# A new instruction order for a 9000-instruction encoder kernel: same work, other places in the queues

## The chip, the cores and the metric

One core of a Trainium2 chip runs the whole kernel as one program. The metric is the time of one execution on the device in microseconds (us). Before the change it was 1069.17 us, the median of 3 runs (1068.3 to 1069.39). The profile shown below comes from one more execution, with its own time.

## The reference: one layer of a hybrid encoder

The input x has 512 rows (the sequence) of 1024 columns, all in float32. What must come out is

```python
h = rmsnorm(x, mix_norm)
p = h @ w_in                                   # 1024 -> 9248 columns
rx, ry, qkv, z, ba, gates = split(p)
y_rnn = rglru_branch(rx, ry, ...) @ w_rnn_proj # 12 blocks of 128 channels, conv of 4, two gates, scans both ways
y_dn  = deltanet_branch(qkv, z, ba, ...) @ w_dn_proj   # 8 heads, chunked delta rule, both ways
g_rnn, g_dn = split(sigmoid(gates))
x = x + (g_rnn * y_rnn + g_dn * y_dn) @ w_out
gt, up = split(rmsnorm(x, ffn_norm) @ w_gate_up)       # 2 x 2816 columns
x = x + (silu(gt) * up) @ w_down
return rmsnorm(x, final_norm)
```

## The kernel before

**Products.** A float32 matrix product is made of three products of a faster type, `float32r`. Each operand is split into a high part (a cast) and a low part (the operand minus its high part). For weights the tiles are called `whi` and `wlo`, for the normalised x `hh` and `hl`; the kernel adds `whi*hh`, `whi*hl` and `wlo*hh` in PSUM. ScalarE makes the casts, VectorE the subtractions, TensorE the products and the transposes. `stage` loads a raw weight tile (`wraw`, three buffers, mostly 512 KB) on SyncE's (SP's) queue, casts it and subtracts. `whi` and `wlo` have two buffers each. PSUM has three buffers `mm`, three `ax` and two `st`.

**Stages.** Two chunks of 128 rows of x are loaded, squared and summed, scaled (half of the columns on VectorE, half on ScalarE), transposed on TensorE into `ax` and evicted as `hh` (ScalarE) and `hl` (VectorE); then the other two chunks (`norm_scale`, `norm_transpose`). From then on the blocks of the recurrent branch (`rg_front`, `rg_exp`, `rg_rest`, `rg_out`: Sigmoid, Tanh and Exp, Sqrt, Gelu), the heads of the delta branch (`dn_front`, `dn_mats`, `dn_inverse`, `dn_state`: Silu, Square, Sqrt, Exp, small 32x32 and 64x64 products) and the output projections run mixed with one another until some 690 us; then the FFN, whose gate/up and down products use seven products of quarter size instead of eight, and the final norm. The first `wraw` tiles are numbers 265 (cast 266, subtraction 267) and 451 (cast 452). Number 113 loads the weights of beta and the decay gates, 32 columns of `w_in`, so its pieces in DRAM are 128 bytes long (cast 114). The first two chunks of x are numbers 8 and 9, the others 55 and 56.

**What sets the order.** The functions do not emit instructions. Every call goes through `Rec`, which notes engine, function, sources and estimated durations with `Plan.add`, and numbers the instructions from 0 to 8999. All 9000 therefore have line 704 in the profile. At the end the list `ORDER` says in which order they are emitted:

```python
with tc.manual_schedule():
    todo = plan.order()
    for i in todo:
        plan.ops[i][1]()
```

`Plan.order` only checks that the list holds each number once and no use ahead of its source. Each engine works off its own instructions in the order in which they are emitted, so `ORDER` fixes five queues: TensorE (5973 instructions), VectorE (1578), ScalarE (1064, eleven of them DMA issues), GpSimd (89, nine of them DMA issues) and SP (296, all DMA issues). Between engines, semaphores make an instruction wait for its sources; an instruction that waits holds up everything behind it on its queue. The durations in `Rec.__getattr__` and the sets in `Plan.TABLES` are not read when the kernel runs.

**ScalarE's tables.** Exp, Sigmoid, Sqrt, Ln, Silu and Gelu sit in different table sets. Where the next function on the queue is not in the loaded set, the compiler puts an `ACT_TABLE_LOAD` ahead of it. Copy, Square, Identity and Abs need none, Tanh is in several sets. How many loads there are is thus a matter of ScalarE's order alone.

Of the kernel before, what the change touches and what calls it, by code (L numbers as in the profile page):

```python
# [31 lines left out]
    8, 10, 9, 265, 111, 110, 99, 112, 100, 2, 5, 101, 0, 103, 104, 106, 102, 1, 5475, 13, 14, 15, 3, 7, 18, 17, 19,  # L32
    266, 16, 39, 11, 12, 20, 21, 22, 267, 31, 23, 24, 25, 26, 29, 27, 30, 28, 32, 33, 34, 35, 36, 37, 38, 40, 41,
    42, 43, 44, 45, 46, 47, 48, 49, 50, 51, 53, 52, 54, 55, 57, 58, 56, 62, 59, 60, 451, 452, 63, 64, 268, 269, 270,
    271, 107, 272, 273, 274, 275, 276, 277, 278, 279, 280, 281, 282, 283, 105, 284, 285, 286, 287, 288, 289, 108,
    290, 291, 454, 455, 456, 457, 458, 459, 460, 65, 67, 68, 75, 76, 69, 316, 317, 318, 319, 453, 66, 61, 70, 77,
    73, 78, 71, 81, 79, 74, 72, 109, 82, 80, 461, 462, 463, 464, 465, 466, 467, 468, 469, 470, 471, 472, 473, 474,
    475, 83, 84, 85, 86, 91, 92, 93, 94, 87, 89, 88, 95, 90, 96, 97, 98, 292, 293, 476, 477, 294, 295, 296, 297,
    298, 299, 478, 300, 301, 302, 303, 304, 305, 306, 307, 187, 583, 502, 503, 504, 188, 308, 309, 310, 311, 312,
    313, 314, 315, 479, 480, 505, 320, 481, 482, 483, 484, 190, 191, 192, 193, 485, 486, 487, 488, 489, 194, 195,  # L40
    490, 196, 197, 491, 492, 493, 198, 199, 200, 201, 494, 495, 202, 203, 204, 205, 496, 497, 498, 499, 500, 321,
    322, 323, 189, 324, 325, 239, 238, 501, 334, 206, 240, 241, 113, 114, 506, 326, 335, 338, 339, 327, 328, 207,
    340, 208, 341, 329, 209, 210, 211, 212, 213, 214, 215, 216, 217, 507, 508, 115, 509, 510, 511, 336, 337, 330,
    331, 332, 333, 218, 219, 220, 221, 222, 223, 224, 116, 117, 118, 225, 226, 227, 228, 512, 229, 119, 529, 584,
    585, 611, 610, 612, 613, 520, 230, 231, 521, 522, 523, 120, 232, 233, 234, 586, 587, 235, 236, 237, 242, 243,
    516, 121, 122, 513, 514, 123, 124, 524, 588, 125, 126, 517, 518, 519, 244, 245, 246, 525, 526, 589, 515, 395,
    394, 343, 396, 342, 247, 397, 527, 528, 127, 128, 129, 130, 131, 132, 133, 590, 591, 134, 256, 135, 136, 137,
    138, 248, 249, 250, 139, 140, 141, 142, 143, 592, 144, 145, 146, 147, 344, 251, 148, 345, 257, 252, 593, 594,
    595, 258, 259, 253, 596, 597, 598, 599, 346, 600, 601, 149, 150, 151, 152, 260, 153, 158, 556, 557, 558, 160,
    154, 155, 159, 559, 161, 530, 347, 348, 254, 261, 349, 262, 350, 263, 264, 351, 352, 602, 603, 353, 604, 605,  # L50
    354, 532, 533, 606, 607, 608, 609, 255, 531, 162, 614, 163, 165, 166, 615, 787, 788, 789, 790, 616, 617, 355,
    356, 357, 358, 359, 360, 534, 535, 536, 361, 537, 538, 539, 540, 362, 363, 364, 365, 541, 542, 366, 367, 368,
    369, 370, 371, 372, 373, 374, 375, 376, 377, 378, 379, 380, 381, 382, 383, 384, 385, 386, 171, 164, 618, 624,
    387, 388, 389, 390, 391, 392, 167, 168, 169, 170, 173, 172, 174, 393, 175, 6, 176, 177, 4, 178, 179, 619, 625,
    628, 629, 630, 1076, 1077, 398, 399, 181, 760, 841, 842, 843, 180, 626, 631, 627, 1079, 543, 544, 545, 400, 401,
    844, 402, 546, 632, 633, 634, 620, 183, 621, 622, 547, 184, 548, 623, 635, 412, 403, 413, 414, 415, 761, 762,
    416, 417, 418, 419, 636, 420, 404, 405, 549, 406, 407, 550, 551, 408, 409, 410, 411, 422, 425, 421, 1080, 1081,
    552, 763, 553, 554, 764, 765, 766, 555, 1082, 767, 768, 769, 1083, 1084, 1085, 1086, 770, 1087, 1088, 1089,
    1090, 1091, 771, 772, 430, 560, 432, 426, 561, 562, 563, 564, 565, 1078, 773, 1092, 774, 775, 776, 777, 778,
    779, 574, 780, 781, 1093, 1094, 782, 566, 575, 576, 783, 895, 896, 424, 423, 1045, 897, 429, 431, 1046, 567,  # L60
    784, 785, 786, 568, 791, 428, 427, 569, 577, 898, 1047, 792, 793, 794, 795, 796, 1095, 1096, 1097, 1048, 1049,
    1050, 1098, 1099, 1051, 1052, 1100, 1053, 1054, 1101, 1102, 1055, 1056, 1057, 1058, 1059, 1060, 578, 579, 570,
    571, 572, 1200, 637, 1103, 1104, 1105, 1106, 1201, 1202, 805, 580, 581, 582, 573, 1061, 806, 807, 1062, 1063,
    808, 433, 439, 638, 185, 1064, 1203, 809, 810, 1204, 1205, 1206, 1207, 801, 1065, 1208, 1209, 1210, 797, 1066,
    802, 1211, 1067, 1068, 1212, 1213, 1069, 1070, 1071, 434, 440, 435, 437, 639, 436, 441, 442, 445, 446, 1214,
    640, 641, 798, 799, 642, 643, 1215, 1216, 1072, 800, 1217, 644, 1218, 645, 803, 804, 646, 647, 1219, 648, 814,
# [1850 lines left out]
```

## Time and profile before

| | before |
|---|---|
| median of 3 runs | 1069.17 us |
| the profiled execution's own time | 1068.94 us |
| its span | 1067.2 us |
| TensorE busy | 1043.8 us, 98% |
| VectorE busy | 897.2 us, 84% |
| ScalarE busy | 680.5 us, 64% |
| GpSimd busy | 48.8 us, 5% |
| ScalarE table loads | 71 |

The span runs from the first to the last instruction; 1.74 us of the execution's time lie outside it. Busy time of TensorE counts bars that overlap: a matmul's bar lasts longer than the distance to the next one's start, so that a busy TensorE need not be one at its full pace. In a row, the part behind `[` is the idle time ahead of the instruction on its engine and what ended it. Names of tiles stand without buffer numbers.

### The profile page before, as it was taken

Reading aid. Unit: us, or ns where it says so; the run is one execution under the profiler, and the core shown is the slowest. Engines: PE = TensorE matmul, PEld = TensorE weight load, DVE = VectorE, ACT = ScalarE, POOL = GpSimd, SP = SyncE. Lnnn points to the kernel's source line nnn. Section 1 sums busy time; section 2 is a strip of 40 time slices with the busy share of each in tenths; the row PEclk is TensorE's granted clock in tenths of the full one; section 3 lists DMA queues with packets and bytes.
Section 4 is the critical chain, followed back from the end, with each engine's and each line's share of the span. In section 5 each row is a group of like instructions: output and inputs, shape, how many; then the busy total and the mean of one; then the engine's idle time right before and its main releaser. Section 6 shows DMA issues by size and latency. Waiting matters only on the chain.

```text
span 1067.2 us, 17684 instructions
## 1 busy us (share of the span) xinstructions
PE 1043.8 (98%) x6730; PEld 907.4 (85%) x6730; DVE 897.2 (84%) x1584; ACT 680.5 (64%) x1235; POOL 48.8 (5%) x93
## 2 busy tenths in 40 slices
PE   6999999999999999999999999999999999999997
PEld 5888887888877978898888878889999999998785
DVE  5668899779997999889949957879889998899877
ACT  6698899898447756857855453438444545355656
POOL 2000002010300100210200000000000000000000
PEclk9999999999999999999999999999999999999999
DMA  6343333236645756453221322632333433336564
GB/s 183 85 109 100 99 95 114 80 117 203 184 117 164 266 168 212 130 180 99 60 57 40 89 66 88 180 99 80 99 99 100 119 99 90 110 116 194 168 220 162
DMA packets 174053, 134.36 MB, mean 126 GB/s; under 512 B 6096, under 2 KB 152704, under 8 KB 173968
## 3 DMA queue, kind: packets, MB, share of 16 engines
q1 hardware_dynamic: 172416, 129.91, 41.2%
q10 hardware_dynamic: 1264, 3.19, 0.9%
q8 instruction: 53, 0.87, 0.4%
q0 software_dynamic: 288, 0.13, 0.2%
q14 instruction: 32, 0.26, 0.1%
HBM read 119.55 MB, written 13.66 MB: 125 GB/s over the span
## 4 chain that ended last, share of the span: by engine, by line
PE 56%; DVE 4%; ACT 2%; DMA 1%; issue 1%; DVEq 0%; ACTq 0%
PE mm L704 30%; PE ax L704 17%; PE st L704 9%; DVE t L704 2%; ACT t L704 1%; DVE wlo L704 1%; DMA wraw<-in_w_out_dram 1%; DVE na L704 1%; DMA wraw<-dsum 0%; ACT whi L704 0%; DMA wraw<-in_w_dn_proj_dram 0%; ACT L704 0%; ACT ax L704 0%; DVE hh L704 0%; DVE so L704 0%
## 5 line engine op out<-in xcount | busy, mean ns | idle before, releaser
L704 DVE TENSOR_TENSOR t<-t,t 128x512 fp32r<-128x512 f32 (+21 forms) x480 | 251.8, 536 | 33.1 <-ACT t L704 24.1
L704 PE MATMUL mm<-hh,whi 128*128 128x512 f32 (+2 forms) x704 | 241.3, 357 | 1.8 <-ACT whi L704 1.1
L704 ACT CAST whi<-wraw 128x1024 fp32r<-128x1024 f32 (+3 forms) x171 | 165.5, 970 | 120.1 <-PE mm L704 57.4
L704 PE MATMUL mm<-hl,whi 128*128 128x512 f32 (+2 forms) x704 | 241.1, 355 | 0.1
L704 DVE TENSOR_TENSOR wlo<-wraw,whi 128x1024 fp32r<-128x1024 f32 (+3 forms) x170 | 191.2, 1128 | 47.6 <-ACT whi L704 36.1
L704 PE MATMUL mm<-hh,wlo 128*128 128x512 f32 (+1 forms) x688 | 174.6, 354 | 0.0
L704 PEld LDWEIGHTS mm<-hh,whi 128*128 128x128 f32 (+1 forms) x704 | 132.6, 189 | 21.5 <-ACT whi L704 2.2
L704 PEld LDWEIGHTS mm<-hl,whi 128*128 128x128 f32 (+1 forms) x704 | 133.0, 189 | 17.6 <-DVE hl L704 0.3
L704 PEld LDWEIGHTS mm<-hh,wlo 128*128 128x128 f32 x688 | 120.9, 189 | 17.9 <-DVE wlo L704 0.3
L704 PE MATMUL ax<-t,t 32*32 32x32 f32 (+3 forms) x870 | 115.2, 263 | 2.2 <-issue 1.0
L704 ACT CAST t<-t 128x512 fp32r<-128x512 f32 (+3 forms) x117 | 74.7, 653 | 48.4 <-DVE t L704 45.1
L704 ACT ACT_TABLE_LOAD x71 | 91.1, 1283 | 9.6 <-PE mm L704 4.6
L704 PEld LDWEIGHTS ax<-t,t 128*128 128x128 f32 (+1 forms) x870 | 82.8, 153 | 11.2 <-ACT t L704 3.1
L704 PE MATMUL mm<-t,whi 128*128 128x512 f32 x320 | 90.7, 395 | 0.3 <-DVE t L704 0.3
L704 DVE SCALAR_TENSOR_TENSOR t<-mm,par,t 128x511 f32<-128x511 f32 (+1 forms) x108 | 80.2, 745 | 9.8 <-ACT t L704 8.5
L704 PE MATMUL mm<-t,t 128*128 128x256 f32 (+1 forms) x348 | 78.1, 313 | 0.1
L704 PEld LDWEIGHTS mm<-t,whi 128*128 128x128 f32 x320 | 59.3, 188 | 13.7 <-DVE t L704 0.9
L704 PEld LDWEIGHTS mm<-t,t 128*128 128x128 f32 x348 | 58.0, 191 | 4.2 <-ACT t L704 0.4
L704 ACT ACTIVATE t<-t 128x128 f32<-128x128 f32 (+4 forms) x84 | 45.6, 555 | 20.7 <-DVE t L704 20.0
L704 PE MATMUL mm<-t,wlo 128*128 128x512 f32 x160 | 48.9, 393 | 0.0
L704 PE MATMUL ax<-whi,t 128*128 128x512 f32 x137 | 48.3, 392 | 0.2 <-ACT whi L704 0.2
L704 PE MATMUL st<-hh,whi 128*128 128x512 f32 (+1 forms) x112 | 41.7, 377 | 0.0
(211 smaller groups left out, 1817.3 us busy)
## 6 DMA issues: line engine op xcount, KB each, us to landing
wraw<-in_w_in_dram SPq DMA_DIRECT2D x72, 512.0 KB, 4.0
wraw<-in_w_gate_up_dram SPq DMA_DIRECT2D x44, 512.0 KB, 3.9
t<-in_w_down_dram SPq DMA_DIRECT2D x22, 512.0 KB, 5.0
dsum<-t SPq DMA_DIRECT2D x22, 512.0 KB, 5.2
wraw<-dsum SPq DMA_DIRECT2D x20, 512.0 KB, 3.9
wraw<-in_w_down_dram SPq DMA_DIRECT2D x15, 512.0 KB, 4.0
wraw<-in_w_rnn_proj_dram SPq DMA_DIRECT2D x16, 384.0 KB, 3.6
t<-gsum SPq DMA_DIRECT2D x16, 256.0 KB, 4.5
```

The lines of the kernel that those rows point to most:

```text
L704: self.plan.add(e, lambda: real(*a, **kw), outs, ins, occ, lat, tail, table, mode)
```

## The change

Only the list `ORDER` is replaced, lines 31 to 520; every function stays as it is, and so do the 9000 instructions and their numbering. The beginning of the list:

```diff
 ORDER = [
-    8, 10, 9, 265, 111, 110, 99, 112, 100, 2, 5, 101, 0, 103, 104, 106, 102, 1, 5475, 13, 14, 15, 3, 7, 18, 17, 19,
-    266, 16, 39, 11, 12, 20, 21, 22, 267, 31, 23, 24, 25, 26, 29, 27, 30, 28, 32, 33, 34, 35, 36, 37, 38, 40, 41,
-    42, 43, 44, 45, 46, 47, 48, 49, 50, 51, 53, 52, 54, 55, 57, 58, 56, 62, 59, 60, 451, 452, 63, 64, 268, 269, 270,
...
+    9, 8, 265, 2, 99, 6, 0, 5, 111, 103, 102, 104, 100, 105, 18, 10, 1, 19, 112, 110, 4, 106, 3, 101, 20, 21, 7, 22,
+    13, 14, 15, 16, 17, 11, 12, 266, 267, 23, 24, 25, 26, 27, 28, 29, 30, 31, 32, 33, 34, 35, 37, 36, 38, 39, 40,
+    41, 42, 43, 44, 45, 46, 268, 47, 48, 49, 50, 51, 53, 52, 54, 451, 113, 452, 55, 57, 56, 583, 316, 317, 62, 63,
...
```

Read by queues, this is what the places named later come to. The lists are cut to one engine each; `+` is the new order of the same queue.

```diff
 SP, from the start
-  8 (x0), 9 (x1), 265 (wraw), 55 (x2), 56 (x3), 451 (wraw), 316, 317 (graw), 187 (wraw), 583 (wraw)
+  9 (x1), 8 (x0), 265 (wraw), 451 (wraw), 113 (wraw, 32 columns), 55 (x2), 56 (x3), 583 (wraw), 316, 317 (graw), 187 (wraw)
 ScalarE, from the start
-  10, 1, 5475, 13 (Square x0), 14 (Sqrt), 17 (scale x0), 19 (Sqrt), 266 (cast), 22 (scale x1), 29, 27, 35, 37 (hh)
+  10, 1, 19 (Sqrt), 22 (scale x1), 13 (Square x0), 14 (Sqrt), 17 (scale x0), 266 (cast), 27, 29, 35, 37 (hh)
 ScalarE, around the Sigmoid at 67.30 us of the old profile
-  398 (Identity), 843 (cast), 180 (Exp), 631, 627 (Sigmoid), 402 (cast)
+  180 (Exp), 396 (cast), 398 (Identity), 627, 631 (Sigmoid), 402 (cast)
 ScalarE, around the Silu at 183.00 us
-  1013 (cast), 1233, 1234 (Silu), 1495 (cast)
+  1329 (cast), 1495 (cast), 1599 (Identity), 1232, 1233 (Silu)
 ScalarE, around the cast at 386.44 us
-  2492 (Square), 2496 (Sqrt), 2888 (copy of na), 3368 (cast whi), 3363, 2886
+  2486, 2490 (Square), 3368 (cast whi), 2882, 2888 (copies of na)
 ScalarE, around the cast at 564.81 us
-  3960, 4941 (Sigmoid), 5028 (cast whi), 4001
+  3960, 4941 (Sigmoid), 5028 (cast whi), 4001
```

On GpSimd's queue the mask `upi`, from which VectorE makes the identity for the transposes, moves behind eight of the nine DMA issues. On SP's queue 211 of 296 entries change places, by 3.0 places on average; on TensorE's 2776 of 5972 pairs of neighbours stay neighbours, on VectorE's 298 of 1577, on ScalarE's 161 of 1063. The last 17 instructions of TensorE are the same.

970 rows, old and new, of the table ORDER are left out of this document.

## The prediction, made before the result was known

> **What bounds the kernel now.** I read the page's totals first, then busy time by stretches, TensorE's waits, the groups of instructions by form, and last the timelines around each wait.
>
> ```profile
> span 1067.2 us, 17684 instructions
> ...
> PE 1043.8 (98%) x6730; PEld 907.4 (85%) x6730; DVE 897.2 (84%) x1584; ACT 680.5 (64%) x1235; POOL 48.8 (5%) x93
> ...
> PE 56%; DVE 4%; ACT 2%; DMA 1%; issue 1%; DVEq 0%; ACTq 0%
> ```
>
> TensorE is busy 98% of the span, and in the chain that ended last VectorE has only 4% and ScalarE 2%. The change removes no matmul, so at most 1067.2 − 1043.8 = 23.4 us of its visible idle time is open to it, and a new order can only move that idle time. The stretches show where it lies (columns: stretch, length, then busy us and count of TensorE, its weight loads, VectorE, ScalarE, GpSimd, then clock, DMA share, GB/s).
>
> ```profile
> 7.50:27.00 19.50, 17.05 (x103) 15.00 (x104) 14.87 (x33) 13.11 (x29) 1.41 (x3) 1.00 0.67 177
> ...
> 100.00:200.00 100.00, 99.57 (x435) 80.93 (x434) 90.86 (x105) 90.44 (x120) 5.59 (x3) 1.00 0.34 96
> ...
> 700.00:1000.00 300.00, 300.00 (x2221) 287.17 (x2220) 265.37 (x447) 153.82 (x270) 0.00 (x0) 1.00 0.38 112
> ...
> 1059.00:1067.20 8.20, 0.30 (x2) 0.00 (x0) 3.99 (x12) 3.29 (x10) 0.00 (x0) 0.71 0.38 133
> ```
>
> Of the 23.4 us, 19.50 − 17.05 = 2.45 lie between 7.5 and 27 us and 8.20 − 0.30 = 7.9 after 1059 us, in the final norm; up to 7.5 lie ahead of 7.5 us, while x is loaded. The stretch from 700 to 1000 us, in the FFN, has none. What is left between 27 and 1059 us is a handful of waits:
>
> ```profile
> PE mm L704 <- ACT whi L704: 1.6, 3, 0.6
> PE ax L704 <- issue: 1.0, 1, 1.0
> PE ax L704 <- ACT t L704: 0.9, 1, 0.9
> PE ax L704 <- DVE t L704: 0.6, 3, 0.3
> PE mm L704 <- DVE t L704: 0.6, 2, 0.3
> ```
>
> ScalarE causes 1.6 + 0.9 = 2.5 us of these in four waits, VectorE 0.6 + 0.6 = 1.2 us in five. An idle time shown is less than what the wait costs, because a matmul's bar overlaps the next one:
>
> ```profile
> 385.86 0.39 PE L704 MATMUL mm<-hh,whi 128*128 128x512 f32 x1
> ...
> 386.54 0.39 PE L704 MATMUL mm<-hl,whi 128*128 128x512 f32 x1
> 387.54 0.50 PE L704 MATMUL mm<-hh,whi 128*128 128x512 f32 x1 [0.61 <-ACT whi L704]
> 387.87 0.39 PE L704 MATMUL mm<-hl,whi 128*128 128x512 f32 x1
> ```
>
> Three starts take 386.54 − 385.86 = 0.68 us, so the pace is 0.227 us. The wait made 1.00 us of it, 0.77 lost against 0.61 shown, and the next start took 0.33, another 0.10. I count waits by starts below.
>
> **The change part by part.** Every instruction stays, only places in the five queues move: 5507 of TensorE's 5973, 1400 of VectorE's 1578, 932 of ScalarE's 1064, by 10.6, 5.4 and 7.2 places on average.
>
> *ScalarE's table loads.* Counting along ScalarE's queue how often the function leaves the loaded set gives 70 for the old list and 60 for the new one (Exp 21 to 15, Sigmoid 17 to 14, Sqrt 14 to 13).
>
> ```profile
> L704 ACT ACT_TABLE_LOAD x71 | 91.1, 1283 | 9.6 <-PE mm L704 4.6 <-DVE so L704 2.5 <-PEq L1903 1.4
> ```
>
> The trace has 71, so the count is right to one. Ten fewer at 1283 ns are 12.8 us less ScalarE work. But ScalarE is busy 64%, so nearly all of it falls into its idle time and is worth nothing; it counts only where TensorE waits behind a load. There are three places where the new list takes away what was in front of the late ScalarE result. At 387.54 us, the weights' high half (number 3368) came late:
>
> ```profile
> 382.69 1.28 ACT L704 ACT_TABLE_LOAD   x1 [2.05 <-DVE so L704]
> ...
> 386.01 0.40 ACT L704 COPY t<-na 32x256 f32<-32x256 f32 x1 [1.72 <-DVE na L704]
> 386.44 1.04 ACT L704 CAST whi<-wraw 128x1024 fp32r<-128x1024 f32 x1
> ```
>
> It stood behind a Sqrt with its table load and behind a copy that waited 1.72 us for VectorE's `na`. In the new list cast 3368 stands directly ahead of these `na` copies and the Sqrt (2496) is no longer among the six instructions ahead of it: 0.77 us gone. At 68.04 us:
>
> ```profile
> 66.29 0.84 PE L704 MATMUL ax<-t,t 128*128 128x512 f32 x3
> 68.04 0.49 PE L704 MATMUL ax<-t,t 128*128 128x512 f32 x1 [0.91 <-ACT t L704]
> ```
>
> ```profile
> 64.36 1.28 ACT L704 ACT_TABLE_LOAD   x1
> 65.66 0.33 ACT L704 ACTIVATE ge<-ax 128x192 f32<-128x192 f32 x1
> 66.00 1.28 ACT L704 ACT_TABLE_LOAD   x1
> 67.30 1.26 ACT L704 ACTIVATE t<-ax,par 128x512 f32<-128x512 f32 x2
> ```
>
> The last of the three starts at 66.29 + 0.84 − 0.39 = 66.74, so the wait cost 68.04 − 66.74 − 0.227 = 1.07 us. The gate's Exp sits between two loads right ahead of the Sigmoid; in the new list a graw cast (396) and a conv start (398) lie between Exp (180) and Sigmoid, and the Exp comes earlier against TensorE. I take the whole 1.07. At 185.16 us:
>
> ```profile
> 184.21 0.84 PE L704 MATMUL mm<-hh,wlo 128*128 128x512 f32 x3
> 185.16 0.50 PE L704 MATMUL ax<-t,t 128*128 128x512 f32 x1
> ```
>
> The last start of the three is 184.66, so 185.16 − 184.66 − 0.227 = 0.27 us; the cast it needs (1495) stood behind a Silu load with two Silus and now stands ahead of them. Sum: 0.77 + 1.07 + 0.27 = **2.1 us**. A wait that stays is this one:
>
> ```profile
> 563.02 1.28 ACT L704 ACT_TABLE_LOAD   x1 [4.63 <-PE mm L704]
> 564.32 0.60 ACT L704 ACTIVATE t<-mm 128x512 f32<-128x512 f32 x1
> 564.81 1.04 ACT L704 CAST whi<-wraw 128x1024 fp32r<-128x1024 f32 x1
> ```
>
> Sigmoid 4941 and cast 5028 are neighbours in both lists. Bounds for the stage between 27 and 1059 us: if all nine ScalarE and VectorE waits went, 2.5 + 1.2 shown, with 0.77 − 0.61 = 0.16 hidden in each and 0.10 behind each as at 387.54, that is 3.7 + 9 × 0.26 = 6.0 us gained. The other end is a loss: one VectorE instruction (90.86 / 105 = 0.87 us) more in front of TensorE in seven places, 6.1 us. I stay at the three waits whose cause the list visibly removes.
>
> *The head.* The first weight cast went ahead of the copy that scales the second 128 rows of x:
>
> ```profile
> 10.00 1.04 ACT L704 CAST whi<-wraw 128x1024 fp32r<-128x1024 f32 x1 [1.32 <-DMA wraw<-in_w_in_dram]
> 10.95 0.72 ACT L704 ACTIVATE t<-t,rin 128x512 f32<-128x512 f32 x1
> ...
> 16.23 1.06 ACT L704 ACTIVATE t<-t 128x1024 f32<-128x1024 f32 x1
> ```
>
> ScalarE idled 1.32 us for the weights, and then the copy, the transposes and ScalarE's evictions `hh` ran late, for which VectorE waited:
>
> ```profile
> 14.23 0.88 DVE L704 SCALAR_TENSOR_TENSOR hl<-ax,gain,hh 128x256 fp32r<-128x256 f32 x2 [0.54 <-ACT hh L704]
> 15.65 0.48 DVE L704 SCALAR_TENSOR_TENSOR hl<-ax,gain,hh 128x256 fp32r<-128x256 f32 x1 [0.54 <-ACT hh L704]
> 16.38 0.87 DVE L704 SCALAR_TENSOR_TENSOR hl<-ax,gain,hh 128x256 fp32r<-128x256 f32 x2 [0.25 <-ACT hh L704]
> ```
>
> The new list has both scaled copies ahead of that cast. VectorE's weight subtraction still comes before its first `hl`, so what can go are its three waits: 0.54 + 0.54 + 0.25 = **1.3 us** earlier for the last `hl` and the matmuls that read it. The upper end is all of TensorE's idle time there, 2.45 us; the lower one is the transfers. SP's queue now issues a second 512 KB weight tile and the 128 KB beta/gate weights (number 113) ahead of rows 2 and 3 of x.
>
> ```profile
> DMA packets 1124, 0.57 MB, mean 283 GB/s; under 512 B 29, under 2 KB 1122, under 8 KB 1124
> ```
>
> That is the stretch from 12 to 14 us: the x rows come in 4 KB pieces and almost none are left, so they had landed by about 12 us. The added 0.524 MB at 283 GB/s are 1.9 us, and the 0.131 MB between 0.5 us at the same rate and 3.3 us at 40 GB/s, the slowest slices that moved much in the old list's stretch with this load (26 to 34 us, slices of 0.2 us):
>
> ```profile
> GB/s 0 0 0 0 0 0 0 0 0 0 0 13 172 338 261 164 284 158 139 184 129 40 40 27 19 0 0 0 0 0 0 0 0 0 0 0 44 113 108 95
> DMA packets 1724, 0.47 MB, mean 58 GB/s; under 512 B 1072, under 2 KB 1724, under 8 KB 1724
> ```
>
> So the rows land between 14.4 and 17.2 us. The Square of them started at 16.23 and should start at 14.9: covered at the near end, up to 2.3 us late at the far one, which would turn 1.3 us of gain into 1.0 of loss. Most slices of that stretch ran at 129 to 338 GB/s, so I take the near end. Behind x, SP's third weight buffer is now taken, so the next weight load waits until VectorE has subtracted the first tile, as SP's queue did before.
>
> The Trainium skill, "DMA: Bandwidth & Descriptors" (Specifications), wants at least 512 B a piece for full rate; the beta/gate load has 128 B pieces, and the 1072 small packets in the slow slices agree. By that rule the head loses 1.0 and the sum would be 1067.8.
>
> *GpSimd and the end.* GpSimd's mask for the identity now follows eight DMA issues; I put the identity at the same 7 to 8 us, between 0.3 late and nothing. In the last 8.2 us the 17 final TensorE instructions keep their order, two ScalarE ones swap: 0, within ±0.2.
>
> *Sum*, against the profiled execution, 1068.94 us (span 1067.2 and 1.74 around it, 0.2 under the median of 1069.17): 1068.94 − 2.1 − 1.3 = **1065.5 us**.
>
> **The rivals.** *Nothing gained* (about 1068.3): the waits only change places. For it: 5507 moved places leave few neighbours as they were, and ScalarE's 36% idle time swallows table loads. Each of the three waits is replaced by one of its like and the head alone gives half, 1068.94 − 0.6. Against: each of the three has lost its visible cause. *Late x rows*: the far end above, 1068.94 − 2.1 + 1.0 = 1067.8. *Most waits go* (about 1061.6): 1068.94 − 1.3 − 6.0 = 1061.6. For it, no wait beyond 27 us exceeds 1.0 us; against, neighbours such as 4941 and 5028 stay.
>
> *VectorE becomes the bound* (about 1071.6, slower): from 100 to 200 us VectorE is busy 90.86 us and has 9 us to spare. The new list places its work in other blocks against TensorE's. If TensorE asks for a result one VectorE instruction earlier than it is ready, that is 0.87 us; seven places cost 6.1, and 1068.94 − 3.4 + 6.1 = 1071.6. It decides from four places on (3.4 / 0.87), where the gain is used up. Against: VectorE causes only 1.2 us of TensorE's waits now, at 91% busy in this stretch.
>
> **How the numbers follow.** Forecast 0.42, its own range 1064 to 1067 (half the three waits, or the head's upper end); nothing gained 0.16; late x rows 0.10; most waits go 0.13; VectorE 0.19. A measurement here tells about 0.2%, 2.1 us, from no change: faster is under 1067.0, slower over 1071.3. Faster: 0.41 of the forecast's, 0.13 and 0.02 of the late rows', 0.56. Slower: VectorE's share and 0.01 of the second, 0.20. The same: 0.24. The range 1060.5 to 1071.5 leaves out half of VectorE's case and the end of the best, about 0.15.
>
> **What would show it.** Right: 61 table loads; no `ACT whi` wait at the group that began at 387.54, none on `ACT t` at the one at 68.04; the first `hh` before 11.2 us and the last of the eight `hl` ending near 15.9 instead of 17.25. Wrong: x's second Square waiting for a DMA past 16 us; `PE <- DVE wlo` or `DVE t` rows of several us between 100 and 500 us, or TensorE's waits in the middle summing to 4.7 us again.

## The result, and the profile after

The new list takes 1059.62 us (median of 4 executions, 1059.15 to 1060.07) against 1068.76 us (1068.3 to 1069.39) for the old one, which has one execution more here than in the table ahead: a ratio of 0.9914, 95% interval 0.9897 to 0.9931, or 9.1 us less. The forecast was 1065.5 us and its range began at 1060.5, so the sign was right and the gain was more than twice the size forecast. The profiled execution took 1060.07 us, its span is 1058.3 us, 8.9 less than before.

The page's totals after, the chain that ended last, and the group of table loads:

```profile
span 1058.3 us, 17715 instructions
...
PE 1037.6 (98%) x6730; PEld 910.3 (86%) x6730; DVE 897.5 (85%) x1584; ACT 665.9 (63%) x1225; POOL 49.1 (5%) x93
...
PE 64%; DVE 7%; issue 1%; ACT 1%; POOL 0%; DMA 0%; DVEq 0%; POOLq 0%
...
L704 ACT ACT_TABLE_LOAD x61 | 78.3, 1283 | 3.2 <-PEq L1903 1.4
```

The loads are down from 71 to 61 as counted. TensorE has the same 6730 instructions, and yet its busy time fell by 6.2 us, from 1043.8 to 1037.6. A matmul that is held up gets a longer bar, not only an idle time in front of it (0.50 us against 0.39 at 387.54 us in the prediction's rows); the waits view sees only the second.

The stretches after (columns as in the prediction), and below them one of before that it did not show:

```profile
100.00:200.00 100.00, 100.00 (x443) 82.81 (x442) 92.90 (x108) 89.24 (x119) 0.03 (x1) 1.00 0.36 98
...
300.00:400.00 100.00, 100.00 (x730) 85.36 (x729) 87.39 (x193) 65.11 (x152) 1.24 (x2) 1.00 0.58 184
...
700.00:1000.00 300.00, 299.59 (x2219) 286.65 (x2218) 269.43 (x450) 158.32 (x275) 0.00 (x0) 1.00 0.38 112
...
1050.40:1058.30 7.90, 0.18 (x1) 0.00 (x0) 4.12 (x13) 3.33 (x10) 0.00 (x0) 0.84 0.47 162
```

```profile
300.00:400.00 100.00, 98.94 (x720) 82.82 (x719) 87.97 (x183) 62.96 (x145) 4.46 (x10) 1.00 0.56 176
```

The counts of TensorE's instructions tell more than its busy time: in the same hundred microseconds it now does 8 more (100 to 200 us) and 10 more (300 to 400). As one list runs ahead of the other, the same hundred microseconds do not hold quite the same instructions; the table further down compares at equal work. The FFN and the last 7.9 us are as they were. The granted clock is 1.00 in all of these but the last.

TensorE's waits between 27 and 1050 us after (us in total, times, longest):

```profile
PE mm L704 <- DVE t L704: 1.6, 2, 1.0
PE mm L704 <- ACT hh L704: 0.5, 1, 0.5
PE mm L704 <- ACT whi L704: 0.5, 1, 0.5
PE ax L704 <- ACT whi L704: 0.4, 1, 0.4
PE ax L704 <- POOL t L704: 0.3, 1, 0.3
```

They sum to 3.3 us against 4.9 before (the prediction's five rows and one of 0.2). The view thus accounts for 1.6 us of a gain of nine.

To find the rest I followed each TensorE instruction through both traces. Between two kinds of instruction the distance from start to start hardly varies when nothing is late (0.227 us between products of 512 columns). The sum of these usual distances is the work done; at equal work the two traces' clocks can be compared:

| TensorE work done, us | time in the old trace | the new list is ahead by |
|---|---|---|
| 12 | 26.9 | 1.2 us |
| 50 | 65 | 0.0 |
| 75 to 100 | 92 to 117 | 1.6 |
| 200 | 218 | 3.4 |
| 300 | 320 | 2.2 |
| 400 | 424 | 4.35 |
| 550 | 580 | 6.5 |
| 650 | 683 | 8.05 |
| 900 | 934 | 8.5 |

Added up over all starts beyond 27 us, TensorE lost 21.4 us against its usual distances before and 13.1 after. Starts more than 0.17 us late made 10.3 us in 25 places before and 5.4 us in 11 after. TensorE instructions whose last operand from another engine was ready less than 1 us ahead of them went from 808 to 221: the new list has more slack everywhere, not only three repairs. This describes the two traces; the experiments below ask what brings it about.

The head after, in TensorE's, ScalarE's and VectorE's timelines (start, length, engine, instruction, idle time before it and what ended it):

```profile
20.48 1.47 PE L704 MATMUL ax<-ident,t 128*128 128x128 f32 x12
...
26.64 0.38 PE L704 MATMUL mm<-hh,whi 128*128 128x256 f32 x1 [0.51 <-ACT hh L704]
```

```profile
9.04 1.03 ACT L704 CAST whi<-wraw 128x1024 fp32r<-128x1024 f32 x1
10.11 0.47 ACT L704 ACTIVATE hh<-ax,gain 128x256 fp32r<-128x256 f32 x1
...
15.38 1.05 ACT L704 CAST whi<-wraw 128x1024 fp32r<-128x1024 f32 x1
16.32 1.07 ACT L704 ACTIVATE t<-t 128x1024 f32<-128x1024 f32 x1
...
18.11 1.34 ACT L704 ACTIVATE t<-t,rin 128x512 f32<-128x512 f32 x2
```

```profile
12.27 0.48 DVE L704 SCALAR_TENSOR_TENSOR hl<-ax,gain,hh 128x256 fp32r<-128x256 f32 x1 [0.54 <-ACT hh L704]
13.00 1.27 DVE L704 SCALAR_TENSOR_TENSOR hl<-ax,gain,hh 128x256 fp32r<-128x256 f32 x3 [0.25 <-ACT hh L704]
14.81 0.48 DVE L704 SCALAR_TENSOR_TENSOR hl<-ax,gain,hh 128x256 fp32r<-128x256 f32 x1 [0.54 <-ACT hh L704]
15.54 0.88 DVE L704 SCALAR_TENSOR_TENSOR hl<-ax,gain,hh 128x256 fp32r<-128x256 f32 x2 [0.24 <-ACT hh L704]
...
26.63 0.48 DVE L704 SCALAR_TENSOR_TENSOR hl<-ax,gain,hh 128x256 fp32r<-128x256 f32 x1 [0.54 <-ACT hh L704]
```

The first cast, now behind both scaled copies, starts at 9.04 instead of 10.00 us, the first `hh` starts at 10.11 us, and the last of the first eight `hl` ends at 15.54 + 0.88 = 16.42 us instead of 17.25. VectorE's waits for `hh` ahead of these eight are still there, 0.54 + 0.25 + 0.54 + 0.24 = 1.57 us against 1.33 before. And the last `hl` of rows 2 and 3 starts at 26.63 us, where it started at 25.98 in the old list; at 26.64 us TensorE waits for an `hh` of the same rows.

The table's 1.2 us at 12 us of work must be read with care, since that mark lies between two losses. By 24 us the new list has begun 54 products of 256 columns against 50, which at 0.12 us from start to start is a lead of 0.5 us. Then the old list loses 0.9 us on its own late rows (starts at 25.34, 25.50, 26.00, 26.52 and 26.74 us, where 0.12 us apart is usual), just ahead of the mark, and the new list loses 1.1 us on its own at 26.64 and 27.16, just behind it.

### The profile page after: what moved, and what is told of

Read it like the earlier page. It is cut to its first block, busy times and chain, and to the rows that moved or that the text cites. A ratio compares the mean times of both kernels' runs of the same rounds, so it can differ in the third digit from the quotient of the medians.

```text
span 1058.3 us, 17715 instructions
## 1 busy us (share of the span) xinstructions
PE 1037.6 (98%) x6730; PEld 910.3 (86%) x6730; DVE 897.5 (85%) x1584; ACT 665.9 (63%) x1225; POOL 49.1 (5%) x93
## 4 chain that ended last, share of the span: by engine, by line
PE 64%; DVE 7%; issue 1%; ACT 1%; POOL 0%; DMA 0%; DVEq 0%; POOLq 0%
PE mm L704 36%; PE ax L704 18%; PE st L704 10%; DVE t L704 5%; DVE wlo L704 1%; DVE na L704 1%; POOL t L704 0%; ACT t L704 0%; DMA wraw<-in_w_down_dram 0%; ACT whi L704 0%; ACT rst L704 0%; DVE rin L704 0%; DVEq L1912 0%; DVE so L704 0%; DVE n L704 0%
## 5 line engine op out<-in xcount | busy, mean ns | idle before, releaser
L704 DVE TENSOR_TENSOR t<-t,t 128x512 f32<-128x512 f32 (+20 forms) x480 | 254.3, 539 | 14.2 <-ACT t L704 7.9
L704 PE MATMUL mm<-hh,wlo 128*128 128x512 f32 (+1 forms) x688 | 169.3, 355 | 0.0
L704 PE MATMUL ax<-t,t 32*32 32x32 f32 (+3 forms) x870 | 112.4, 261 | 0.0
L704 PE MATMUL mm<-t,whi 128*128 128x512 f32 x320 | 86.4, 393 | 1.0 <-DVE t L704 1.0
L704 PE MATMUL mm<-t,t 128*128 128x256 f32 (+1 forms) x348 | 74.7, 313 | 0.0
L704 PEld LDWEIGHTS mm<-t,whi 128*128 128x128 f32 x320 | 59.5, 188 | 13.7 <-issue 1.4
L704 PE MATMUL ax<-whi,t 128*128 128x512 f32 x137 | 45.4, 391 | 0.4 <-ACT whi L704 0.4
L704 PE MATMUL mm<-t,wlo 128*128 128x512 f32 x160 | 44.3, 392 | 0.0
```

The costliest lines, as they stand in the source:

```text
L704: self.plan.add(e, lambda: real(*a, **kw), outs, ins, occ, lat, tail, table, mode)
```

## The experiments

All kernels below are one of the two lists with instructions moved, except two which add ScalarE instructions. In them the list takes fewer lines, and the line of all instructions is 679 instead of 704. In the expectations theory L is that the ten table loads carry the gain, theory P that TensorE reaches freshly made operands later in its own order, theory C that the five queues have to fit each other and no single one carries it; S, T and R are explained where they first stand. Times in brackets after a ratio are the 95% interval against the old list.

### Fewer loads, and later uses, in the old list

**e1_loads**: old list, five ScalarE functions moved in seven steps, so that 63 loads are left.

```diff
 ScalarE
-1612 (Sigmoid) ... 2049 (Exp), 1543
+2049 (Exp), 1612 (Sigmoid) ... 1543
 ... likewise 2485 (Silu) later, 3279 (Silu) earlier, 5026 (Sigmoid) later, 4474 (Exp) later
```

> The old list with seven ScalarE instructions (3631, 4496, 2049, 5026 twice, 2485, 4474) moved by 1 to 9 places on ScalarE's queue beside others of their table set, so that its table loads go from 71 to 63; the other four queues stay the old ones word for word. Theory L (the 9.1 us come from the ten fewer table loads): eight of ten loads give 8/10 of the gain, about 7 us, so about 1061.5. Theory P (they come from TensorE reaching freshly made operands later in its queue; loads in ScalarE's idle time are worth nothing): within 1 us of the old list, 1068 to 1069.

Measured: 1073.14 us, 1.0038 (1.0023 to 1.0053), slower than either theory said. More than the whole loss is in one place, where a product waited for a PSUM bank that VectorE had not emptied yet (TensorE's timeline and, below it, the stretch behind it):

```profile
506.01 0.77 PE L679 MATMUL mm<-hh,whi 128*128 128x512 f32 x1 [2.86 <-DVE t L679]
506.57 0.63 PE L679 MATMUL mm<-hl,whi 128*128 128x512 f32 x1
507.00 0.63 PE L679 MATMUL mm<-hh,whi 128*128 128x512 f32 x1
```

```profile
506.00:508.00 2.00, 1.99 (x5) 1.61 (x6) 1.83 (x6) 0.00 (x0) 0.00 (x0) 0.50 0.11 31
```

The wait cost 2.9 us and then as much again: the granted clock went to 0.50 until 512 us and the products came 0.43 us apart. Everywhere else the kernel is within some 1 us of the old list, and the waits at 68, 185 and 387 us stand. Eight loads taken out bring nothing here; but none of the eight lay between 65 and 200 us, where ScalarE is fullest and the new list has three fewer.

**e2_pe_late**: old list, TensorE's order alone changed.

```diff
 TensorE, at 53 places where an operand came late: 184 matmuls with operands long ready go ahead of the waiting one
-3319, 3370, 3371, 3372, 3373, 3374, 3320, 3321, 3322, 3323
+3319, 3320, 3321, 3322, 3323, 3370
```

> The old list with TensorE's queue alone changed: at 53 places where the old trace shows a matmul that started less than 1 us after its last operand from another engine was ready and lost time there, up to four independent matmuls from later are put in front of it (184 matmuls moved). 71 table loads as before. By starts, those 53 places lost 6.6 us in the old trace, 4.3 of them in 16 waits. Theory P: most of it comes back, 4 to 7 us, so 1062 to 1065. Theory L: nothing beyond 1 us, about 1068.

**e3_both**: the two together.

> The two edits together (63 loads, 184 matmuls moved). If both act on their own places the gains add: theory P 1062 to 1065 as with the second edit alone; theory L about 1061.5 as with the first alone; both causes about half each: some 4 us below each single edit.

Measured: 1092.51 us, 1.0222 (1.0205 to 1.0239), and 1095.33 us, 1.0244 (1.0229 to 1.0259), both slower. In e2 the old waits at 387.54 and 565.90 us go and the one at 68 us stays (0.91 us at 68.48). What was put behind is late for the next engine, which hands the lateness on, as in a wait of 2.06 us for ScalarE at 477.64. Theory P in this simple form falls: slack for one operand, bought by a delay of another, is no gain.

### The price of a load

**e4_hidden** and **e5_tight**: new list with ten loads added, by pairs of tiny activations on a spare tile that nothing reads; the outputs stay as they are. In e4 they follow instructions behind which ScalarE idles, in e5 they stand ahead of work that TensorE needs at once.

```diff
+        extra = {2843: (AF.Sqrt, AF.Exp), 5272: (AF.Sqrt, AF.Sigmoid), 4748: (AF.Sqrt, AF.Sigmoid), 4802: (AF.Sqrt, AF.Sigmoid), 7794: (AF.Sqrt, AF.Silu)}
         for i in todo:
             plan.ops[i][1]()
+            for fn in extra.get(i, ()):
+                nc.scalar.activation(warm, eps_t, fn)
```

In e5 the pairs follow 430, 737, 4679, 5363 and 5404.

> The new list with ten table loads put back: after five ScalarE instructions behind which ScalarE was idle for 3.8 to 5.4 us in the new trace (2843, 5272, 4748, 4802, 7794), two one-column activations on a spare tile, the first from another table set, the second back. Ten loads and ten small activations, about 15 us of ScalarE time. Theory P: within 0.5 us of the new list, 1059.1 to 1060.2. Theory L, if a load costs wherever it stands: most of the 9 us is given back, about 1068.

> The new list with ten table loads put back as in the run with hidden loads, but in front of urgent work: the five pairs of one-column activations stand behind ScalarE instructions 430, 737, 4679, 5363 and 5404, where the next cast is due on TensorE 0.9 to 1.4 us after it ends and ScalarE is not idle. A pair costs 2.97 us; less what each has in hand, 1.85 + 1.67 + 1.74 + 1.9 + 2.09 = 9.2 us. Theory S (a ScalarE or VectorE instruction costs TensorE exactly what it comes too late at its place, whatever the number of loads): 1065 to 1069. If a load is worth nothing at all: 1059.6.

Measured: e4 1059.64 us, 0.9913 (0.9898 to 0.9927), 0.0 against the new list; e5 1073.70 us, 1.0048 (1.0033 to 1.0063), 14.1 more and above the 1065 to 1069 of theory S. The row of TensorE's waits of e5 beyond 27 us that stands first:

```profile
PE mm L679 <- ACT whi L679: 6.3, 4, 2.3
```

A load, here with a tiny activation behind it, has no price of its own: 0 in an idle time, 1.4 us on average in front of an urgent result, of which 0.17 is the clock (0.50 for some 3.4 us after the wait at 666 us, 1.7 us in all).

**e17_new_loads**: new list; five ScalarE functions go one place earlier, back into the order to each other that the old list has. That brings ten loads back and moves nothing else.

```diff
 ScalarE
-445 (Sqrt), 573 (Sigmoid)      866 (Sigmoid), 737 (Exp)
+573 (Sigmoid), 445 (Sqrt)      737 (Exp), 866 (Sigmoid)
 ... likewise 804 (Sigmoid) ahead of 741 (Exp), 862 (Sigmoid) ahead of 742 (Sqrt), 1711 (Gelu) ahead of 2048 (Exp)
```

> The new list with five neighbouring pairs on ScalarE's queue swapped back into the order that the old list has (445 Sqrt, 741 Exp, 866 Sigmoid, 742 Sqrt, 2048 Exp, each past one neighbour of another table set): ten table loads come back (71), nothing else moves. Four of the five places lie between 60 and 135 us, where ScalarE is some 90% busy, the fifth near 265 us. If the saved loads make the new list's gain in that part (3.4 us by starts up to 218 us, 1.5 of it between 65 and 90 us): 2.5 to 8 us slower than the new list, 1062 to 1068. If they are worth nothing there either, as those put into ScalarE's idle time: 1059.1 to 1060.1.

Measured: 1071.58 us, 1.0025 (1.0016 to 1.0034): 12.0 us more than the new list, slower than the old one and above the 1062 to 1068 expected. At equal work nothing is lost until 95 us, 10.3 us between there and 150, and 1.2 at some 290. ScalarE's timeline and TensorE's waits from 27 to 700 us show it, then the stretch from 100 to 145 us in e17 and in the new list:

```profile
117.02 1.28 ACT L679 ACT_TABLE_LOAD   x1
118.32 0.72 ACT L679 ACTIVATE t<-t,rgs 128x512 f32<-128x512 f32 x1
```

```profile
PE ax L679 <- ACT t L679: 5.1, 4, 2.1
```

```profile
100.00:145.00 45.00, 40.45 (x173) 31.49 (x172) 35.93 (x42) 44.12 (x55) 0.00 (x0) 1.00 0.26 74
```

```profile
100.00:145.00 45.00, 45.00 (x200) 37.27 (x199) 43.27 (x48) 43.48 (x58) 0.03 (x1) 1.00 0.33 88
```

ScalarE has no idle time before either of the two. It is busy 43.48 of 45.00 us even in the new list, 97%, so each load put in pushes everything behind it back, and TensorE gets through 173 instructions instead of 200. Of the 12.0 us, 1.7 are the clock again (0.52 from 150 to 152 us, 0.62 to 154, after a wait of 2.08 us at 149.28); the other 10.3 make 1.0 us a load over the ten. Each swap also puts one function behind another, so this is the price of a swap with its two loads, halved.

**e18_new_loads_late**: new list with six loads put back, two each at some 345, 520 and 553 us, where ScalarE is busy 64 or 65% of the hundred microseconds around.

```diff
 ScalarE
+2838 (Exp) ahead of 2699 (Silu); 3290 (Sqrt) ahead of 4365 (Silu); 4475 (Exp) ahead of 4941 (Sigmoid)
```

> The new list with six table loads put back between 340 and 565 us, where ScalarE is 50 to 85% busy, by small moves on ScalarE's queue towards the old order (Exp 2838 two places earlier at 348 us, Silu 4365 one later at 518 us, Exp 4475 three earlier at 553 us; the sources of all three are ready in time): 67 loads. If a load costs by how full ScalarE is: little here, less than 0.5 us each, so 1059.5 to 1062.5. If each costs about 1.2 us as the ten put back at 95 to 250 us did on average: about 1067.

Measured: 1063.75 us, 0.9951 (0.9934 to 0.9967), 4.1 us more than the new list and above the 1059.5 to 1062.5 expected: 0.7 a load, the clock's share in it. Two of the pairs cost, 3.7 us at 345 to 358 (1.7 of it the clock) and 2.3 at 530 in the profiled execution, the one at 553 us nothing. TensorE's waits of e18, and the three places in the new list:

```profile
PE st L679 <- ACT t L679: 1.8, 1, 1.8
PE ax L679 <- POOL t L679: 1.6, 1, 1.6
```

```profile
330.00:350.00 20.00, 20.00 (x313) 16.72 (x313) 9.98 (x12) 18.93 (x42) 0.00 (x0) 1.00 0.52 163
520.00:535.00 15.00, 14.72 (x245) 11.76 (x244) 11.68 (x20) 12.90 (x39) 6.26 (x14) 1.00 0.27 68
540.00:560.00 20.00, 20.00 (x152) 18.83 (x151) 11.21 (x35) 7.92 (x17) 0.00 (x0) 1.00 0.10 28
```

Over these 15 or 20 us ScalarE is busy 95%, 86% and 40% in the new list, and only the last pair is free.

So in these runs the price goes by what ScalarE has to spare at that place, not by its share of the span. Neither kernel puts the loads exactly where the old list had its extra ones: e17 has 13 between 100 and 150 us, the new list 8, the old list 7.

### Repairs in one list

**e6_old_repaired**: old list; 13 late instructions of ScalarE, VectorE and the DMA queue go a place or two earlier, and three products of TensorE a few places later. **e7_new_repaired**: new list; the same at its two new VectorE waits and one for GpSimd.

```diff
 e6, ScalarE
-2496 (Sqrt), 2888 (copy of na), 3368 (cast whi), 3363
+3368 (cast whi), 2496 (Sqrt), 2888 (copy of na), 3363
 ... likewise 180, 869, 3051, 4001 and 5028, 5599, 8611, 8665; VectorE 1969, 3747
 e7, VectorE
+2541 ahead of 2105, 3428 ahead of 2107, 2108
```

> The old list with 13 late instructions (12 places on ScalarE's and VectorE's queues between 68 and 1013 us: 631, 627, 869, 1969, 3368, 3051, 3747, 5028, 4001, 5599, 8611, 8646, 8629) each put one or two places earlier on its own queue, ahead of work that is not waited for; TensorE's queue is the old one but for 7 places, table loads are two more than before. Theory S: the 13 waits hold 6.0 us by starts in the old trace; about 4 to 6 us back, 1063 to 1065.5. Rival C (only the new list as a whole works, single repairs hand the wait on to the next place): within 1.5 us of the old list, 1067.5 to 1070.

> The new list with three instructions put one or two places earlier on their own queues: VectorE's 2541 and 3428, the conv steps that free a PSUM buffer `mm` for which TensorE waited at 290.20 (1.14 us by starts) and 294.80 us (0.76 us), ahead of small updates of the triangular inverse, and GpSimd's memset 3749 (0.35 us at 532.39). Theory S: 1.1 + 0.4 + 0.35 = about 1.9 us less, 1057.5 to 1058.2. Rival C: within 0.5 us of the new list, 1059.1 to 1060.1.

Measured: e6 1078.18 us, 1.0088 (1.0073 to 1.0103), 9.3 us slower than the old list; e7 1059.32 us, 0.9913 (0.9898 to 0.9928), the new list's time within the spread. In e6 some of the repaired waits go (387.54, 565.90), others stay or grow (0.70 us at 534.99, 1.84 at 1019.66), and new ones come (1.03 at 69.34, 1.47 at 396.02, 1.13 at 689.46), so that it ends up slower than both of its expectations. In e7 the wait at 290.20 us is gone and its instruction's neighbour is late:

```profile
291.10 1.66 PE L679 MATMUL mm<-t,wlo 128*128 128x512 f32 x6 [0.83 <-DVE wlo L679]
```

### One engine's order alone

**e9_old_pe_new**: old queues, TensorE's new order as far as the buffers allow. **e10_old_rest_new**: TensorE's old order, the other queues as far towards the new one as they can go. **e11_new_pe_old**: new queues, TensorE near its old order. **e12_new_actdve_old**: new list, ScalarE and VectorE as far towards the old one as they can go.

```diff
 e9:  ScalarE, VectorE, GpSimd, SP as in the old list
-     TensorE as in the old list
+     TensorE in the new order where the buffers allow it (5524 of 5972 neighbours of the new list)
```

> The old list with TensorE's queue alone turned to the new order, pair by pair of neighbours as far as sources and buffers allow (33636 of 38205 swapped pairs done, 5462 of 5973 instructions moved); the other four queues are the old ones, 71 table loads. Theory T (TensorE's order carries the gain): 4 to 8 us faster than the old list, 1061 to 1065. Theory R (the order of ScalarE and VectorE carries it): no gain, 1068 to 1070. Theory C (neither alone, the queues have to fit each other): slower than the old list, over 1071.

> The mirror of it: the old list with the queues of ScalarE, VectorE, GpSimd and SP turned to the new order as far as TensorE's old queue, sources and buffers allow (of swapped pairs 57% done on ScalarE, 79% on VectorE, 96% on GpSimd, 57% on SP); 73 table loads, so the ten saved loads are not among it. Theory R: 4 to 8 us faster than the old list. Theory T: no gain. Theory C: slower than the old list, over 1071.

> The new list with TensorE's queue alone turned back to the old order (32564 of 38205 pairs), the other queues new, 61 table loads. Theory T: the gain is given back, 1066 to 1069. Theory R: most of it stays, 1060 to 1063. Theory C: slower than both lists, over 1071.

> The new list with ScalarE's and VectorE's queues turned back to the old order as far as possible (73% and 84% of the swapped pairs), TensorE's, GpSimd's and SP's queues new; 72 table loads, eleven more than the new list. Theory R: the gain is given back, 1066 to 1069. Theory T: most of it stays, 1060 to 1063, and the eleven loads with it. Theory C: slower than both lists, over 1071.

Measured: 1234.12 us, 1.1534 (1.1513 to 1.1556); 1279.33 us, 1.1972 (1.1951 to 1.1993); 1190.33 us, 1.1132 (1.1112 to 1.1152); 1261.23 us, 1.1811 (1.1773 to 1.1849). None of these mixtures shows any of the gain, as theory C said. They say little more: the mixtures are 120 to 210 us off, part of it the clock, whose mean over the span fell to between 0.948 and 0.977, and none of them is a clean exchange of one queue. What one queue alone would bring in buffers that fit it is not shown.

### One list, then the other

**e8_new_then_old**: new list's first 1550 instructions (to some 220 us), the others in the old order. **e15_new_old**: new list for 4870 (to some 601 us), then old. **e16_old_new**: the old list for the same 4870, then new.

```diff
 e15
-    todo: old list
+    todo: first 4870 of the new list, then those left in the old list's order
```

> The first 1550 entries of the new list (to about 217 us of the old profile), then the rest in the old order. By starts at equal work the new list is 3.4 us ahead there, 0.0 of it in the first 40 us. Theory S, gains of single places that add: 1065.0 to 1066.5, with the wait at 68.04 us gone and that at 387.5 us still there. Rival C: about 1068 to 1070, as the old rest absorbs it.

> The new list's first 4870 entries (to about 601 us of the new profile, 608 of the old; only two instructions change sides), then the old order. 61 table loads, since all ten saved ones lie in this part. By starts at equal work the new list is 6.9 us ahead there. If the gain is made place by place and kept: 1062 to 1062.5. If the old rest takes it back (theory C over the whole list): above 1066.

> The mirror: the old list's first 4870 entries, then the new order; 71 table loads. If the gain is made place by place: 8.9 - 6.9 = 2.0 us less than the old list, about 1066.9, although no table load is saved. If the saved loads are the cause of all of it: 1068.9.

Measured: e8 1067.79 us, 0.9992 (0.9982 to 1.0001); e15 1061.21 us, 0.993 (0.9915 to 0.9945), 7.3 us less than the old list; e16 1067.56 us, 0.999 (0.9981 to 1.0000), 1.0 less with all 71 loads, though its interval reaches 1. e15 and e16 sum to 8.3 of 9.1 us, so the gain is kept piece by piece, and seven eighths of it are made before 601 us. In e8 the trace is 4.1 us ahead at 218 us, and 2.7 of that is lost at the joint itself, where two casts are late, so that its time is no price for the first 220 us.

### The head

**e13_new_head**: new list, the transposes of rows 2 and 3 earlier on TensorE. **e14_new_head3**: that and the moves of e7.

```diff
 TensorE
-460, 461, ... 468 (products), transposes up to 86
+transposes up to 86, 460, 461, ... 468 (products)
 ... likewise 474 to 478 behind the transpose 94
```

> The new list with TensorE's queue changed in the first 28 us alone: the 12 transposes 67 to 86 of rows 2 and 3 of x, which started at 20.48 us behind products while their input was there at 19.05 to 19.45, come 9 matmuls (about 1 us) earlier, and the last four (91 to 94) 5 matmuls earlier. If the head's gain of 1.3 us, there at 12 us of TensorE's work, was given back to these rows' late `hh` and `hl`: 0.8 us less than the new list (1058.8), and the wait at 26.64 us is gone. Rival: the evictions end when they end because of the rows' landing, or the wait moves on: within 0.3 us of the new list.

> The same with the three swaps of 2541, 3428 and 3749 added, which alone gave 0.3 us. If the places are independent: 1.1 us less than the new list, about 1058.5; if waits only move on: 1059.3 to 1059.6.

Measured: e13 1058.76 us, 0.9904 (0.9890 to 0.9919); e14 1058.83 us, 0.9907 (0.9891 to 0.9924). Both have a span of 1056.7 us, 1.6 less than the new list's, and the median is 0.9 less; the spreads still touch. TensorE's and VectorE's timelines of e13:

```profile
19.38 1.50 PE L679 MATMUL ax<-ident,t 128*128 128x128 f32 x12 [0.67 <-DVE t L679]
...
26.10 0.39 PE L679 MATMUL mm<-hl,whi 128*128 128x256 f32 x1
```

```profile
25.56 0.48 DVE L679 SCALAR_TENSOR_TENSOR hl<-ax,gain,hh 128x256 fp32r<-128x256 f32 x1 [0.54 <-ACT hh L679]
```

The last `hl` starts 1.07 us earlier than in the new list, the wait at 26.64 us is gone, and the kernel is 1.1 us ahead of the new list from 28 us on. No kernel ran faster; the moves of e7 add nothing to it.

## Why the prediction was right in sign and wrong in size

**The head (1.3 us): wrong in how, and given back in rows 2 and 3.** The term was the sum of three waits of VectorE for `hh`, which were to go. They did not (1.57 us after, 1.33 before). What came is an earlier start: with the cast at 9.04 us VectorE's weight subtraction begins at 10.10 us instead of 11.08, and the last of the eight `hl` ends 0.83 us earlier, not 1.3. Five traces of kernels with each head differ by 1.33 us at 12 us of work, but that agreement is luck, since the mark lies behind the old list's loss and ahead of the new one's. At 30 us of work the same ten traces differ by 0.2 us, with a spread of 1.3 in each group. The prediction followed the gain to "the matmuls that read" the first eight `hl` and did not ask what is late next: the transposes of rows 2 and 3 stand behind products in TensorE's new order, begin at 20.48 us although their inputs, the scaled copies from 18.11 us, are ready at 19.45, and so the last `hl` comes at 26.63. e13 moved them ahead and gained 1.1 us.

**The rows of x: no transfer was waited for, but the Square did not come earlier.** The second Square was to start at 14.9 us and starts at 16.32, past the 16 us that was to be a sign against. It is no DMA wait: the row shows none, and ScalarE was busy until then with the cast at 15.38, a cast for which the prediction's 14.9 had left no time. The rival of late rows, by the Trainium skill's 512 bytes a piece ("DMA: Bandwidth & Descriptors", Specifications), is not borne out here: the load in 128-byte pieces ahead of x delayed no user of x.

**Ten loads worth nothing: a term put at nothing for a reason that does not hold, and its size stays open.** The prediction priced the loads that it did not see in front of a wait at nothing, since "ScalarE is busy 64%, so nearly all of it falls into its idle time". That is the share of the whole span. e4 shows loads that cost nothing, and e17 ten that cost 12.0 us, more than the whole gain, in a stretch where ScalarE is full. They do not stand where the ten of the old list stood. In two of the stretches where the old list had more loads, ScalarE had little to spare too (old list, then new, columns as above; 5 loads against 4, then 9 against 6):

```profile
65.00:100.00 35.00, 34.01 (x150) 27.45 (x149) 24.03 (x27) 34.61 (x49) 0.64 (x1) 1.00 0.36 99
...
150.00:200.00 50.00, 49.60 (x217) 40.42 (x217) 44.73 (x52) 46.82 (x64) 5.59 (x3) 1.00 0.36 104
```

```profile
65.00:100.00 35.00, 35.00 (x156) 28.85 (x156) 27.72 (x35) 32.80 (x48) 2.08 (x2) 1.00 0.41 114
150.00:200.00 50.00, 50.00 (x222) 41.41 (x221) 44.66 (x56) 40.76 (x55) 0.00 (x0) 1.00 0.34 95
```

ScalarE was busy 99% from 65 to 100 us and 94% from 150 to 200, and is now busy 94% and 82%; TensorE does 6 and 5 instructions more. The prediction had the row for 100 to 200 us in front of it, with ScalarE at 90.44, and read VectorE's column from it. But the loads fell also from 12 to 9 between 200 and 300 us, where ScalarE was busy 75% in the old list, and from 12 to 9 between 500 and 600, at 66%.

That loads put into the new list cost time is shown; that the ten left out of the old one brought as much is not. e1, the only attempt, took out eight others. And the gain does not follow the loads. Between the marks of the table at equal work, the stretches with hardly any load fewer (65 to 117, 320 to 424 and 580 to 683 us of the old trace, with 6 loads against 6, 10 against 9 and 3 against 3) gain 1.6, 2.15 and 1.55 us, 5.3 together. The two with nine fewer (117 to 218 and 424 to 580 us, 18 against 13 and 18 against 14) gain 1.8 and 2.15, 4.0 together. A load left out may pay only further on, so this bounds nothing, but more than half of the gain arose where there was hardly a load less.

**Three waits worth 2.1 us: all three went, one of them for another reason, and with them most of the others.** At 387.54 us the cast now runs at 381.06 and its product starts at 383.68 us, 1.6 us after the cast's end: as forecast. At 185.16 us likewise, the cast is 4.3 us earlier. At 68.04 us the forecast was right by luck:

```profile
67.92 1.27 ACT L704 ACTIVATE t<-ax,par 128x512 f32<-128x512 f32 x2
```

```profile
69.37 0.39 PE L704 MATMUL mm<-hh,whi 128*128 128x512 f32 x1
69.60 0.84 PE L704 MATMUL ax<-t,t 128*128 128x512 f32 x3
```

The operands of the product that waited there had been ready for 6 us; what it lacked was an `ax` bank, which the Sigmoid empties. The Sigmoid comes at 67.92 us, later than the 67.30 of before. The wait is gone because TensorE does products of others until 69.37 us and asks for the bank at 69.60.

**"A wait that stays": wrong.** Sigmoid 4941 and cast 5028 are neighbours in both lists, but the load in front of them is not there any more:

```profile
552.78 0.60 ACT L704 ACTIVATE t<-mm 128x512 f32<-128x512 f32 x1 [0.62 <-PE mm L704]
553.28 1.04 ACT L704 CAST whi<-wraw 128x1024 fp32r<-128x1024 f32 x1
```

The cast is done at 554.3 us and its product starts at 560.55. I had read two neighbours' places and not the table that their predecessors leave behind.

**The middle at 2.1 us, with 6.0 as its bound: the step that failed.** The prediction stayed "at the three waits whose cause the list visibly removes", and bounded the stage by the nine waits of ScalarE and VectorE that the waits view shows, with 0.26 us added to each. Counted by starts the old list lost 21.4 us there and the new one 13.1, so the middle brought 8.3 us where 2.1 were forecast and 6.0 allowed. Starts over 0.17 us late make 4.9 of the 8.3; the rest is lateness too small to stand in the view. Some 6 to 7 us are in both kernels (below) and were not to be had, so the bound should have been about 15 us. The rival that most waits go, at 1061.6, was the nearest to the truth for the wrong sum.

One row of the waits had no price and no reason for having none, `PE ax <- issue`. It is the longest wait of the old list beyond 27 us:

```profile
624.66 0.38 PE L704 MATMUL ax<-t,t 32*32 32x32 f32 x20 [1.04 <-issue]
```

The product's operands from other engines had been ready since 622.34 us. The wait comes in all five kernels that keep the old order around this place (0.58 to 1.21 us: the old list, e1, e6, e8, e15) and in none that has the new order there. So about 1 us of the gain belongs to the order and, as far as the traces show, to no late operand and no load; what TensorE waited for is not shown.

**VectorE as the bound: not decided against the change, but it is there.** Between 200 and 300 us of work lies the one stretch beyond the head with a loss, 1.2 us in the table. TensorE waits there twice for VectorE, whose small updates, subtractions and steps of the convolution from 283.71 to 296.2 us follow each other without an idle time (TensorE's timeline):

```profile
290.20 1.15 PE L704 MATMUL mm<-t,whi 128*128 128x512 f32 x4 [0.98 <-DVE t L704]
...
294.80 0.47 PE L704 MATMUL mm<-hh,whi 128*128 128x512 f32 x1 [0.60 <-DVE t L704]
```

Two places, where it would have taken four to use up the forecast gain. Moving these steps of VectorE a place or two ahead, in e7, only put the wait elsewhere.

**What stays open.** The 8 us beyond the head are shown to be spread over the mixed part up to 690 us, to be kept piece by piece (e15, e16), and to be lost again when ten loads are put into a full stretch. That TensorE's operands have more slack goes with the gain, but no run shows that the slack makes it, and no single queue or repair brought any of it. How it divides between the loads and the rest of the order could not be told: the new list's ScalarE order does not fit the old list's buffers, and with them the mixtures lose far more than is in question.

## What to carry to other kernels

Price an instruction on a helper engine by that engine's idle time in the stretch where it stands, not by its share of the span: the same 1.28 us load cost from nothing to 1.4 us here. Bound what a new order can bring by the starts of the bounding engine against its own usual distances, since the waits view showed 4.9 of 21.4 us. And where a gain is given to one group of instructions, follow it to the next group on each engine: the head's lead was gone at 28 us, and 1.1 us came when the next transposes moved too.

## What the runs showed of the hardware that was not expected

A wait of TensorE can cost twice. After waits of 1.55 us (e5, 666.49), 1.77 (e18, 348.59), 2.06 (e2, 477.64), 2.08 (e17, 149.28) and 2.86 us (e1, 506.01) the granted clock went to 0.50 for 3.4 us, in e1 for twice that, and 1.7 to 3.4 us were lost. After 1.47 us in e6 (396.02), after 1.73, 1.66, 1.74 and 2.25 us in e5 (83.07, 627.08, 686.93 and 135.91) and after 2.84 us in e3 (518.69) it stayed at 1.00. The longest wait of either list beyond 27 us is 1.04 us, and neither has a stretch of 2 us below 0.97 up to 1050 us.

What tells the two kinds apart is where the wait lies. The clock falls on a grid of 3.41 us: in e9 it falls at 59.5, 90.2 and 117.6 us, 9 and 8 times 3.41 apart. In e5 this is the last 3.41 us of the grid ahead of the fall, and the first behind it:

```profile
663.98:667.39 3.41, 1.62 (x7) 0.82 (x6) 0.92 (x2) 2.72 (x6) 0.00 (x0) 1.00 0.01 3
667.39:670.80 3.41, 3.41 (x9) 2.64 (x10) 2.33 (x5) 0.73 (x2) 0.00 (x0) 0.50 0.18 49
```

In the five places where the clock fell, TensorE was busy for 1.26 to 1.64 us of the 3.41 ahead of the fall. In the six where it stayed, each stretch of the grid, stepped off from a fall in the same run, has 1.67 us or more: e3's 2.84 us are split over two, with 2.10 and 1.78 us busy, and e5's 2.25 us likewise, with 2.16 and 2.41. So a wait costs twice when it empties about half of one such stretch, and the same wait may fall on either side of a border. In the mixtures e9 to e12 that limit is less sharp: the clock fell once after a stretch with 2.07 us busy and stayed once after one with 1.46. The Trainium skill ("TensorE: Matmul & The Clock Gate", What's actually happening) puts the drop after at least one idle window of about 3.4 us, in windows that run freely. The grid agrees with such windows; a whole one without work was not needed here.

Both kernels have some 70 to 90 starts that come 0.06 to 0.17 us later than usual with every operand long ready (0.315 us between two products instead of 0.227); they sum to 6 to 7 us in each and no view names a cause.

Behind a table load the next activation starts 1.30 us after the load's start (117.02 and 118.32 in e17). The further 1.38 us that the Trainium skill adds for each switch ("ScalarE: Activation LUTs", What ACT_TABLE_LOAD costs) does not show in these rows.
